# One attention stage, 1369 steps in a hand-written order: the order written anew in its opening and in its last list

## The chip, the cores and the metric

The kernel runs on one core of a Trainium2 chip. Its time is the time that the device takes for one execution, in microseconds (us). A core has several engines with an instruction queue each, and each takes its queue in order: PE (TensorE) multiplies and transposes, ACT (ScalarE) copies, scales and takes exponentials, DVE (VectorE) adds, subtracts and reduces, POOL (GpSimd) and SP (SyncE) here mostly issue DMAs. They wait for one another through semaphores. An engine that stands at an instruction whose input or output buffer isn't ready holds back all that is behind it in its queue, ready or not.

## The reference

One step of a streaming encoder layer, for 1024 prompt tokens and 32 sample tokens with a cache of 512. The part that matters here is branch A, multi-head latent attention with eight heads: queries come from a latent of rank 384, keys and values from one of rank 256, and a rotated key part (krope, 32 wide) is shared by all heads.

```python
q = (rms_norm(q_lat, g_q_lat) @ w_uq).reshape(B, T, H_A, NOPE + ROPE)
q_nope, q_rope = q[..., :NOPE], apply_rope(q[..., NOPE:], cos, sin)
k_rope = apply_rope(k_r, cos, sin)            # also an output of the layer
k_nope, v = c_kv @ w_uk, c_kv @ w_uv          # per head, 64 + 64
s = (einsum('bqhd,bshd->bhqs', q_nope, k_nope) + einsum('bqhr,bsr->bhqs', q_rope, k_rope)) * MLA_SCALE
p = softmax(where(kpos // CHUNK <= qpos // CHUNK, s, NEG))
o_a = einsum('bhqs,bshd->bqhd', p, v)
merged = g_a * (o_a @ w_proj_a) + g_b * (o_b @ w_proj_b)
```

`o_b` is the other branch, finished earlier. The sample's 32 tokens attend to the cache and to themselves.

## The kernel before

All data are float32. A product is made of three matmuls: each operand is split into a high half (rounded, ACT, L68) and a low half (the rest, DVE, L71), and `mm3` multiplies high by high (L75), low by high (L76) and high by low (L77).

The stages follow one another: constants, the common projection, the other branch, the latents, latent attention (`stage_mla`, about 573 to 830 us), the merge of the branches, the feed-forward net. Latent attention takes its eight heads in four pairs; the work of a pair is a *list*, 0 to 3. In a pair, query blocks of 128 go against the keys that they may see.

The order of the work in this stage is written out by hand: `ORDER_M` is a string of tokens, and `mla_attend` takes them one by one and calls a small step for each. The stage runs with a manual schedule for PE, ACT and DVE, so the order of the tokens is the order on those three engines; the orders of POOL and SP follow from the tiles. A token's first digit says whose step it is, its letter which, a last number (as in `f2`) how often it is taken. The tokens that matter:

- `9…`: the first expansion. 9z, 9x, 9y are matmuls for rotated queries, plain queries and keys (352, 352 and 512 columns), 9A a block of values (12 matmuls of 256), 9c and 9d the high and low half of a value block (L1568, L71), 9B the rotation of queries (L1479, its last two issue stores), 9X and 9K the copies of the queries of the two heads (DVE L1498, ACT L1496), 9H/9g and 9L/9b the halves of the keys, 9R and 9r the halves of the key rows that come from krope (`KH<-A`, `KL<-A`), 9J and 9j those of the queries. 9t turns krope for its output (three transposes, L1394), and 9n copies it to a buffer `nat` (L1397, L1398) and stores it with seven POOL DMAs.
- no digit: the other branch's product with `w_proj_b`, of which steps are strewn among the lists: Q fetches its operand, e and l split it (`ObH`, `ObL`), U, W and w load and split weights, f is a product of three matmuls of 264 columns, G copies a finished tile to `nat` (L1889) and stores it to `pbd` (POOL, L1890). There are two `nat` buffers, for 9n and all G together.
- `0…` to `3…`: a list's own steps. S scores (L1619 to L1624), M, m, n maxima, E exponential (L962), R, c, C the scale, T transposes (L806), h and v the halves of the transposed weights (`PTh`, `PTl`, or `ptd` on the diagonal), V the product with the values (L820), o and p its copy and sum (L792, L794). In list 3, q and r split the result for the next stage.
- 3Y: one of the 32 steps of the sample's attention (`mla_sample`), strewn over list 3. In each of its two halves come scores, maximum, exponential, scale, transposes and copies (L1789), product with the cache (L1795), copy (L1798), a last product (L1804; the 31st 3Y in the second half) and its copies `os` (L1809) with their store to `oa` (POOL, L1811; the 32nd).

Behind the last token `stage_mla` loads the attention's result back (`big<-oa`, SP, L1678) as three operands (k = 1, 2, 0), splits them to `QH`/`QL`, `KH`/`KL` and `QH`/`QL`, splits the weights `w_proj_a` (`wh<-KSm`, `wl<-KSm`), and begins the next stage's product with them (352 columns). These steps stand outside the manual schedule: they go where the scheduler puts them, in among the last tokens too.

Of the kernel before, what the change touches and what calls it, by code (L numbers as in the profile page):

```python
# [44 lines left out]
class K:  # L45
# [802 lines left out]


    ORDER_M = """  # L850
        9A 9z 9z 9z 9c 9d 9z 9z 9B 9z 9B 9z 9z 9c 9B 9B 9z 9y 9B 9y 9H 9x 9x 9B 9g 9x 9X 9K 9d 9A 9R 9c 9x 9c 9x
        9r 9y Q 9x 9L 9x 9X 9d 9b 9y 9g 9H Q 9x 9x 9d 9A 9X 9b 9A 9J 9c 9K 9c 9L Q W 9j 9d 0S1.0 9d w 9K 9c Q e
        0M1.0 e l e 0n1.0 0E1.0 l 0S0.0 0M0.0 e 0S1.1 f 9c l 9t 0n0.0 0E0.0 f 9d l 9d 0R0.0 0S2.0a f W 0c0.0
        0S0.1 f G f 0M0.1 0R1.0 f 0n0.1 0E0.1 f2 w 0R0.1 0c1.0 0M1.1 G 9n 0S2.0b 0C0.1 0n1.1 0M2.0b 0E1.1 f
        0M2.0a 0R1.1 f 0m2.0 f 0T0.0 f 0D 0h0.0 f 0E2.0a 0v0.0 0C1.1 0S2.1a 0E2.0b G 9J f 0M2.1a 0S2.1b 0S3.0b
        0V0.0 f 0M2.1b 0m2.1 0E2.1b 0T1.0 0s2.0 0T1.1 f 0S3.0a 0E2.1a f 0h1.0 9j f 0M3.0b 0M3.0a G 0R2.0 0m3.0
        0h1.1 0s2.1 0E3.0a 0R2.1 0S3.1b 0v1.1 f 0M3.1b 0E3.0b 0C2.1 f 0S3.1a 0M3.1a f 0m3.1 0c2.0 0o0 0E3.1a 0p0
        f 0S4.0a 0s3.0 f 0T2.0 G 0S4.0b 0V1.1 0M4.0a 0v1.0 f 0E3.1b 0S4.1b 0h2.0 0V1.0 0M4.0b 0s3.1 0m4.0 0I
        0R3.0 0v2.0 0T2.2 0E4.0a 0R3.1 0i 0T2.1 0M4.1b 0h2.2 0o1 0S4.1a 0p1 0z 0z 0M4.1a 0z G 0h2.1 0z 0E4.0b
        0m4.1 0E4.1a 0v2.2 0c3.0 0S5.0b 0V2.2 0S5.0a 0v2.1 0C3.1 0z 0M5.0b 0V2.1 0T3.3 0z 0M5.0a 0V2.0 0B 0B  # L860
        0h3.3 0m5.0 0z 0z 0B 0z 0B 0x U 9Z 0s4.0 9Z 0v3.3 0o2 0T3.1 0E4.1b W 0s4.1 0T3.2 0h3.2 0x 0B 0p2 0B 0x
        0R4.1 0v3.2 0S5.1b 0X 0V3.3 0E5.0b 0h3.1 0V3.2 0v3.1 0E5.0a 0T3.0 0R4.0 0C4.1 0V3.1 0K 0h3.0 0c4.0 0v3.0
        U 0S5.1a 0x 0M5.1b 0S6.1 0V3.0 0T4.3 0x 0o3 0x 0M5.1a 0x 0s5.0 0m5.1 0T4.2 0h4.3 w 0M6.1 0v4.3 0x 0E5.1b
        0X 0K 0p3 0h4.2 0R5.0 0T4.1 0h4.1 0n6.1 0x U 0v4.2 0E5.1a 0E6.1 0V4.3 0s5.1 0c5.0 0X 0K 0V4.2 0T4.0
        0S6.0 0v4.1 0R5.1 0h4.0 f 0C5.1 0J 0v4.0 f 0M6.0 0S7.0 0n6.0 f 0V4.1 0T5.1 0T5.2 0M7.0 0V4.0 f 0h5.1 0j
        0h5.2 G 0y 0v5.2 f 0E6.0 0R6.1 0y 0n7.0 0o4 f 0R6.0 0H f 0E7.0 f 0T5.0 0p4 0C6.1 0c6.0 0L 0S7.1 0h5.0
        0v5.1 0M7.1 0v5.0 0V5.2 0g 1S1.1 W 0T6.1 G 0n7.1 0V5.1 0h6.1 0R7.0 1M1.1 0b 1n1.1 0E7.1 0V5.0 0y 0o5
        0T6.0 1E1.1 0c7.0 0v6.1 0h6.0 1S0.0 0p5 w 0y 1S1.0 1M0.0 f 0R7.1 0C7.1 0g 0V6.1 f 0H f 0T7.0 1S0.1 0v6.0
        0V6.0 W 1n0.0 f 0b 1E0.0 1S2.0b 1M1.0 0L 1R0.0 1n1.0 f w 1M0.1 1n0.1 1c0.0 0h7.0 1M2.0b 1E1.0 0o6 f
        0v7.0 0p6 1S2.0a 1E0.1 1M2.0a f 1R0.1 f 1R1.0 1m2.0 0J 1C0.1 1S2.1b 0V7.0 G G 0j 1R1.1 f 1M2.1b f 1T0.0  # L870
        0o7 1E2.0b f 1C1.1 1S2.1a 1D U 1M2.1a 1E2.0a 1S3.0a 1m2.1 f2 1c1.0 1h0.0 W 0p7 f 1s2.0 1E2.1a 1T1.0
        1E2.1b 1M3.0a 1S3.0b 1S3.1b 1v0.0 w 1M3.0b G 1V0.0 1m3.0 1s2.1 1R2.0 1T1.1 1h1.0 1o0 f 1R2.1 f 1E3.0a
        1h1.1 G f 1M3.1b 1p0 1S3.1a 1E3.0b f 1c2.0 1v1.0 1k f 1v1.1 1M3.1a 1s3.0 1m3.1 1C2.1 1V1.1 1V1.0 1S4.0a
        1T2.2 f 1E3.1a 1o1 1E3.1b 1p1 1S4.0b 1T2.1 1M4.0a f 1h2.2 1s3.1 G 1R3.0 1R3.1 f 1v2.2 1h2.1 1c3.0 1S4.1b
        1M4.0b f 1v2.1 1T2.0 1m4.0 1C3.1 1V2.2 f 1E4.0a 1h2.0 1S4.1a 1T3.3 1M4.1b 0Z 1v2.0 1I 1V2.1 1V2.0 1M4.1a
        1E4.0b 1m4.1 1h3.3 1v3.3 1E4.1b 1o2 1i 1s4.0 1T3.2 1E4.1a 1S5.0a 1S5.0b 1T3.1 1x 1h3.2 1S5.1b 1p2 1R4.0
        1M5.0b G 1s4.1 1R4.1 1N 1c4.0 1x 1V3.3 1M5.0a 1m5.0 1x 1v3.2 1V3.2 1M5.1b 1x 1C4.1 1E5.0b 1h3.1 1T3.0
        1v3.1 1S5.1a 1X 1E5.0a 1x 1M5.1a 1m5.1 1h3.0 1s5.0 1K 1S6.0 1R5.0 1v3.0 1M6.0 1E5.1b 1T4.3 1E5.1a 1c5.0
        1x 1h4.3 1V3.1 1V3.0 0Z 1T4.2 1x 1X a 1s5.1 1n6.0 1o3 U Q 1h4.2 1K 1v4.3 1R5.1 1E6.0 1C5.1 1v4.2 1p3
        1R6.0 1c6.0 1x 1x 1X 1Z 1J 1j 1K Q 1T4.1 f2 1h4.1 f2 G 1V4.3 1V4.2 1T4.0 1S6.1 1v4.1 1h4.0 1S7.0 f 1y  # L880
        1v4.0 1T5.2 1M7.0 1h5.2 1n7.0 1M6.1 1V4.1 1v5.2 1V4.0 1E7.0 1n6.1 1T5.1 1o4 1h5.1 1E6.1 1y f 1T5.0 f 1H
        1p4 1v5.1 1S7.1 1R7.0 1h5.0 1R6.1 1C6.1 f 1V5.2 1L 1g 1v5.0 1V5.1 1c7.0 2S0.1 1T6.1 e 1M7.1 1b 1V5.0 W
        2M0.1 1n7.1 l 1T6.0 1h6.1 2n0.1 1y 1o5 1p5 1v6.1 1y 1E7.1 1h6.0 1v6.0 1R7.1 2S0.0 2E0.1 1C7.1 8S 1V6.1
        1H 1V6.0 8s a 2S2.0b 1o6 2M0.0 a 2n0.0 G 1T7.0 1h7.0 1p6 1L 2S1.0 8A 2M2.0b 2R0.1 2M1.0 1g 2E0.0 2n1.0
# [30 lines left out]
        3T7.0 G 3v6.0 3h7.0 f 3V6.0 3r f 3v7.0 3o6 3q 3Y 3p6 3r 3V7.0 3o7 f 3Y 3q f3 3p7 3r f 3q f G G 3r
# [1806 lines left out]
```

## Time and profile before

| | us |
|---|---|
| median of three runs (lowest, highest) | 1691.21 (1689.96, 1692.04) |
| the profiled execution | 1692.0 |
| its span in the trace | 1690.2 |
| PE busy in the span | 1647.4 (97%) |
| DVE, ACT, POOL busy | 1268.7, 1007.4, 299.2 |
| from 573 to 835 us: PE busy | 253.43 of 262 |

A row of a timeline gives the start in us from the span's start, the duration in us, the engine, the line, the operation, output tile <- input tiles and the shape; at its end, in brackets, how long the engine had been idle before and what released it. `x4` joins four equal neighbours. A matmul's duration runs over that of the next: its cost to PE is the distance from its start to the next one's. A row of the waits gives the engine, the line and tile that waited, the engine, tile and line that it waited for, then the sum in us, the count, and the longest. A row of the windows gives a stretch of time and the engines' busy time in it. PEclk is the clock that was granted to PE, as a share of full speed.

### The profile page before, as it was taken

To read this page: it belongs to the slowest core of one execution; us is meant where nothing else is said; L and a number is where in the kernel's file an instruction comes from. 1 tells how busy PE (TensorE), PEld (TensorE's weight loads), DVE (VectorE), ACT (ScalarE), POOL (GpSimd) and SP (SyncE) were. 2 spreads that over 40 slices of the span, in tenths; PEclk is the share of its full clock that TensorE was granted. 3 is DMA by queue.
4 is the path that set the end of the run, shared out by engine and by line. 5 is a ranking of instruction groups with operands and counts; after the bars stand their busy time and mean duration, and the time that the engine had idled before them with its cause. 6 is when DMAs were issued, how large, how long until landed. Compare 5 with 4: busy or idle time off the path is not lost. (4 is left out here: it accounts for less than half of the span.)

```text
span 1690.2 us, 30269 instructions
## 1 busy us (share of the span) xinstructions
PE 1647.4 (97%) x11592; PEld 1511.3 (89%) x11592; DVE 1268.7 (75%) x2140; ACT 1007.4 (60%) x1945; POOL 299.2 (18%) x581
## 2 busy tenths in 40 slices
...
DMA packets 194145, 260.62 MB, mean 154 GB/s; under 512 B 23374, under 2 KB 132304, under 8 KB 193936
## 3 DMA queue, kind: packets, MB, share of 16 engines
...
q14 instruction: 54, 0.44, 0.1%
...
## 5 line engine op out<-in xcount | busy, mean ns | idle before, releaser
L68 ACT ACTIVATE wh<-wr 128x1024 fp32r<-128x1024 f32 (+2 forms) x151 | 130.2, 864 | 231.7 <-PE s L2176 83.2
L71 DVE TENSOR_TENSOR wl<-wr,wh 128x1024 fp32r<-128x1024 f32 (+2 forms) x151 | 148.3, 985 | 79.3 <-ACT wh L68 78.9
L75 PE MATMUL mm<-hh,wh 128*128 128x352 f32 x456 | 152.6, 335 | 0.1
L76 PE MATMUL mm<-hl,wh 128*128 128x352 f32 x456 | 148.6, 326 | 0.1
L77 PE MATMUL mm<-hh,wl 128*128 128x352 f32 x456 | 148.4, 325 | 0.0
L2175 PE MATMUL mm<-T,wh 128*128 128x256 f32 (+1 forms) x376 | 108.2, 288 | 0.0
L2177 PE MATMUL mm<-T,wl 128*128 128x256 f32 (+1 forms) x376 | 107.2, 286 | 0.6 <-DVE wl L71 0.5
L2176 PE MATMUL mm<-T,wh 128*128 128x256 f32 (+1 forms) x376 | 106.7, 284 | 0.0
L2177 PE MATMUL s<-T,wl 128*128 128x256 f32 (+1 forms) x348 | 99.3, 285 | 0.0
L2175 PE MATMUL s<-T,wh 128*128 128x256 f32 (+1 forms) x348 | 99.3, 285 | 0.0
L2176 PE MATMUL s<-T,wh 128*128 128x256 f32 (+1 forms) x348 | 98.8, 284 | 0.0
L71 DVE TENSOR_TENSOR wl<-S,wh 128x1024 fp32r<-128x1024 f32 (+1 forms) x55 | 59.2, 1077 | 51.7 <-ACT wh L68 51.4
L75 PEld LDWEIGHTS mm<-hh,wh 128*128 128x128 f32 x456 | 86.4, 190 | 3.7 <-issue 2.1
L2316 DVE SCALAR_TENSOR_TENSOR u<-u,c,u 128x1058 f32<-128x1058 f32 x68 | 87.0, 1317 | 1.9 <-ACT u L2313 0.7
L76 PEld LDWEIGHTS mm<-hl,wh 128*128 128x128 f32 x456 | 86.5, 190 | 2.2 <-DVE hl L333 0.7
L806 PE MATMUL tr<-c,A 128*128 128x128 f32 x576 | 86.7, 272 | 0.6 <-DVE ptd L71 0.6
L77 PEld LDWEIGHTS mm<-hh,wl 128*128 128x128 f32 x456 | 86.3, 189 | 0.6 <-issue 0.4
L68 ACT ACTIVATE wh<-S 128x1024 fp32r<-128x1024 f32 (+1 forms) x55 | 51.8, 943 | 47.9 <-PE s L2176 13.4
L2175 PE MATMUL tr<-T,wh 128*128 128x272 f32 (+1 forms) x272 | 77.8, 286 | 0.0
L2177 PE MATMUL tr<-T,wl 128*128 128x272 f32 (+1 forms) x272 | 77.7, 286 | 0.0
L2176 PE MATMUL tr<-T,wh 128*128 128x272 f32 (+1 forms) x272 | 77.3, 284 | 0.0
L71 DVE TENSOR_TENSOR PTl<-tr,PTh 128x512 fp32r<-128x512 f32 x96 | 65.5, 686 | 11.8 <-ACT PTh L68 11.0
...
## 6 DMA issues: line engine op xcount, KB each, us to landing
...
```

The costliest lines, as they stand in the source:

```text
L68: self.nc.scalar.activation(out, in_, AF.Identity, scale=scale)
L71: return self.nc.vector.tensor_tensor(out, full, hi.bitcast(F32), ALU.subtract)
L75: m(ps, lh, rh, start=start, stop=False)
L76: m(ps, lh, rl, start=False, stop=False)
L77: self.pe = m(ps, ll, rh, start=False, stop=stop).ins
L806: self.nc.tensor.transpose(tr[:, (2 * s + q) * P : (2 * s + q + 1) * P], at[q][:, b * P : b * P + P], self.idt)
L2175: m(ps[:, :n], w[0][:, k], x[0][:, k, c], start=first and k == 0, stop=False, skip_group_check=True)
L2176: m(ps[:, :n], w[0][:, k], x[1][:, k, c], start=False, stop=False, skip_group_check=True)
L2177: i = m(ps[:, :n], w[1][:, k], x[0][:, k, c], start=False, stop=k == 3, skip_group_check=True)
L2316: nc.vector.scalar_tensor_tensor(y, u[:, w : w + YW], self.cvT[:, w, cc : cc + 1], y, ALU.mult, ALU.add)
```

## The change

The change replaces tokens of `ORDER_M` in two stretches: the opening (the first 333 tokens, which are 328 afterwards) and the end of list 2 with list 3 (the last 404, now 402). The 632 tokens between stay word for word. The steps are the same in number and kind; some single f become f2 or f4. No other line changes. Of the table's diff, its first lines:

```diff
     ORDER_M = """
-        9A 9z 9z 9z 9c 9d 9z 9z 9B 9z 9B 9z 9z 9c 9B 9B 9z 9y 9B 9y 9H 9x 9x 9B 9g 9x 9X 9K 9d 9A 9R 9c 9x 9c 9x
+        9z 9z 9z 9z 9z 9z 9B 9z 9y 9z 9z 9B 9B 9x 9B 9A 9x 9A 9B 9x 9B 9c 9x 9x 9y 9d 9X 9c 9c 9R 9d 9c 9x 9g Q
```

ACT in the expansion, first before and then after: the copies of the second head's queries (L1496) and the key rows (`KH<-A`), among halves of values (L1568) and keys.

```order
L1568 ACTIVATE V_7006<-mm_7016 128x4x64
L1568 ACTIVATE V_7007<-mm_7016 128x4x64
L68 ACTIVATE KH_6987<-mm_7068 64x512
L68 ACTIVATE KH_6989<-mm_7068 64x512
L1496 ACTIVATE big_7094<-s_7078 64x352
L68 ACTIVATE KH_6987<-A_6222 64x1024
L1568 ACTIVATE V_7006<-s_7100 128x4x64
L1568 ACTIVATE V_7007<-s_7100 128x4x64
```

```order
L1568 ACTIVATE V_7007<-mm_7060 128x4x64
L1568 ACTIVATE V_7006<-s_7076 128x4x64
L68 ACTIVATE KH_6987<-A_6222 64x1024
L1568 ACTIVATE V_7007<-s_7076 128x4x64
L68 ACTIVATE KH_6989<-mm_7043 64x512
L68 ACTIVATE KH_6987<-mm_7043 64x512
L1496 ACTIVATE big_7111<-s_7055 64x352
L1496 ACTIVATE big_7111<-s_7097 64x352
```

The key rows stood behind the first of these query copies; now all three query copies stand behind the key rows and the first key halves.

ACT at the krope output (L1397, L1398) and the first copies of finished tiles (L1889), before and after; all of them write the two `nat` buffers.

```order
L971 ACTIVATE A_7221<-A_7221,sum_7223 128x128
L1889 COPY nat_7282<-mm_7239 128x264
L962 ACTIVATE A_7271,sum_7273<-s_7274,mx_7272,lat_6225 128x256
L971 ACTIVATE A_7197<-A_7197,sum_7199 128x384
L1889 COPY nat_7306<-mm_7285 128x264
L1397 COPY nat_7309<-tr_7245 128x256
L1398 COPY nat_7309<-tr_7245 8x128
L962 ACTIVATE A_7231,sum_7233<-s_7234,mx_7232,lat_6225 128x512
```

```order
L68 ACTIVATE KH_6989<-s_7151 64x512
L1568 ACTIVATE V_7006<-s_7162 128x4x64
L1397 COPY nat_7187<-tr_7145 128x256
L1398 COPY nat_7187<-tr_7145 8x128
L1568 ACTIVATE V_7007<-s_7162 128x4x64
L68 ACTIVATE ObH_7223<-A_7124 128x528
L68 ACTIVATE ObH_7223<-A_7155 128x528
L68 ACTIVATE wh_6993<-wr_7010 128x512
L962 ACTIVATE A_7198,sum_7200<-s_7201,mx_7199,lat_6225 128x256
```

The krope copies stood behind two L1889; now they stand ahead of the first one, inside the expansion.

ACT at the end of the sequence, before and after: the last diagonal weights (`ptd`), the copies of results (L792), and the next stage's operands `KH<-big` (k = 2) and `QH<-big` (k = 0) and weights `wh<-KSm` (of which before has the first just ahead of these rows).

```order
L68 ACTIVATE ptd_6982<-tr_10417 128x384
L792 COPY o_10439<-pv_10412 64x256
L68 ACTIVATE V_9588<-o_10398 64x256
L792 COPY o_10454<-pv_10449 64x256
L68 ACTIVATE V_9588<-o_10439 64x256
L68 ACTIVATE V_9588<-os_9739 128x32
L68 ACTIVATE V_9588<-o_10454 64x256
L1889 COPY nat_10482<-mm_10426 128x264
L68 ACTIVATE wh_10547<-KSm_10508 128x512
L1889 COPY nat_10485<-mm_10466 128x264
L68 ACTIVATE KH_6987<-big_10500 128x1056
L68 ACTIVATE QH_10494<-big_10504 128x1056
```

```order
L1889 COPY nat_10421<-mm_10374 128x264
L68 ACTIVATE KH_6987<-big_10500 128x1056
L68 ACTIVATE ptd_6982<-tr_10430 128x384
L792 COPY o_10443<-pv_10425 64x256
L68 ACTIVATE V_9577<-o_10399 64x256
L68 ACTIVATE QH_10494<-big_10504 128x1056
L1889 COPY nat_10463<-mm_10439 128x264
L68 ACTIVATE wh_10513<-KSm_10508 128x512
L792 COPY o_10466<-pv_10457 64x256
```

`KH<-big` and `QH<-big` stood behind all steps of the list; now they stand among the last of them, `KH<-big` right ahead of the last `ptd`. On DVE the low halves `KL<-big` and `QL<-big` stand in the same places: `KL` right ahead of the last `ptd`, `QL` ahead of `wl<-KSm`.

In the tokens, the sample's last two steps (31st and 32nd 3Y) stood 17 and 11 places from the end (`3o6 3q 3Y 3p6 3r 3V7.0 3o7 f 3Y 3q f3 3p7 3r f 3q f G G 3r`), and stand 73 and 64 places from it now, ahead of the scores of the last block and half of the last products with the values. The other thirty are spread anew over list 3.

More of the change, by code (lines that the diff above doesn't have):

```diff
@@ L856 @@
[L856 to L860, printed above, removed]
@@ new lines @@
+        9x 9x 9x 9H 9K 9d 9r 9X 9K 9L 9t 9X 9K 9y Q 9y 9J 9A 9H 9d 9b 9j 9L Q Q 9g 9c 9n 9b 0S0.1 9c 0M0.1 9A 9d
+        9d e e W 0n0.1 0E0.1 l l w e 0S1.0 e 0S0.0 0M0.0 W l l 0n0.0 0M1.0 0E0.0 0S1.1 0n1.0 0M1.1 f2 0R0.1
+        0R0.0 f2 G 0n1.1 0C0.1 0S2.0a f 0E1.0 9c 0M2.0a 0c0.0 f 0S2.0b 9d 0E1.1 0M2.0b 0R1.0 0m2.0 w 9c f2 0T0.0
+        0E2.0a 0R1.1 0E2.0b 9d 0S3.0a 0s2.0 0C1.1 0S2.1a 0h0.0 0S2.1b f2 0R2.0 f 0M2.1a G 0c1.0 0T1.0 0v0.0 f2
+        0M2.1b 9J U 0m2.1 0E2.1b 0M3.0a 0D 9j f 0E2.1a G 0h1.0 f 0S3.0b f 0V0.0 0M3.0b G 0m3.0 0S3.1b 0E3.0a
@@ new lines @@
+        0s2.1 f 0o0 0v1.0 0T1.1 f 0M3.1b 0S3.1a f 0R2.1 0M3.1a f 0m3.1 0E3.0b 0c2.0 0C2.1 0h1.1 f2 0E3.1a f
+        0s3.0 f 0p0 0T2.1 0S4.0b 0S4.0a 0v1.1 0E3.1b 0I 9Z G 0S4.1b 0V1.1 0R3.0 0s3.1 0M4.0b 0V1.0 0i 0h2.1
+        0M4.0a 0T2.2 0c3.0 0o1 0z 0z 0h2.2 0z G 0m4.0 0E4.0b 0v2.1 0T2.0 0M4.1b 0R3.1 0p1 0z 0h2.0 0v2.2 0C3.1
+        0S4.1a 0M4.1a 0v2.0 0m4.1 0V2.2 0E4.0a 0T3.3 0h3.3 0S5.1b 0v3.3 0V2.1 0V2.0 0M5.1b 0T3.2 0E4.1a 0z 0T3.1
+        0B 0h3.2 0z 0B 0S5.0a 0E4.1b 0z 0h3.1 0v3.2 0o2 0s4.0 0B 0B 0R4.0 0S5.0b 0x 0s4.1 0z 0p2 0M5.0b 0c4.0 W
@@ new lines @@
+        0R4.1 0V3.3 0V3.2 0z 0M5.0a 0m5.0 0v3.1 0E5.0b 0x 0T3.0 0h3.0 0V3.1 0x 0B 0B 0C4.1 0E5.0a 0S5.1a 0T4.3
+        0v3.0 0T4.2 0V3.0 0X 0x 0h4.3 0v4.3 0M5.1a 0m5.1 0o3 0x 0S6.1 0p3 0h4.2 0T4.1 0E5.1a 0h4.1 0V4.3 0v4.2
+        0K 0V4.2 0M6.1 0x 0E5.1b 0s5.0 0R5.0 0X 0s5.1 0n6.1 w 0R5.1 0x 0x 0x 0X 0T4.0 0v4.1 0c5.0 0K 9Z 0h4.0
+        0E6.1 0S6.0 f 0C5.1 0J U 0v4.0 f 0M6.0 0S7.0 0n6.0 f U 0K 0V4.1 0T5.1 0T5.2 0M7.0 0V4.0 f 0h5.1 0j 0h5.2
+        G 0y 0v5.2 f 0E6.0 0R6.1 0y 0n7.0 0o4 f 0R6.0 0H f 0E7.0 f 0T5.0 0p4 0C6.1 0c6.0 0L 0S7.1 0h5.0 0v5.1
@@ new lines @@
+        0M7.1 0v5.0 0V5.2 0g 1S1.1 W 0T6.1 G 0n7.1 0V5.1 0h6.1 0R7.0 1M1.1 0b 1n1.1 0E7.1 0V5.0 0y 0o5 0T6.0
+        1E1.1 0c7.0 0v6.1 0h6.0 1S0.0 0p5 w 0y 1S1.0 1M0.0 f 0R7.1 0C7.1 0g 0V6.1 f 0H f 0T7.0 1S0.1 0v6.0 0V6.0
+        W 1n0.0 f 0b 1E0.0 1S2.0b 1M1.0 0L 1R0.0 1n1.0 f w 1M0.1 1n0.1 1c0.0 0h7.0 1M2.0b 1E1.0 0o6 f 0v7.0 0p6
+        1S2.0a 1E0.1 1M2.0a f 1R0.1 f 1R1.0 1m2.0 0J 1C0.1 1S2.1b 0V7.0 G G 0j 1R1.1 f 1M2.1b f 1T0.0 0o7 1E2.0b
+        f 1C1.1 1S2.1a 1D U 1M2.1a 1E2.0a 1S3.0a 1m2.1 f2 1c1.0 1h0.0 W 0p7 f 1s2.0 1E2.1a 1T1.0 1E2.1b 1M3.0a
@@ new lines @@
+        1S3.0b 1S3.1b 1v0.0 w 1M3.0b G 1V0.0 1m3.0 1s2.1 1R2.0 1T1.1 1h1.0 1o0 f 1R2.1 f 1E3.0a 1h1.1 G f 1M3.1b
+        1p0 1S3.1a 1E3.0b f 1c2.0 1v1.0 1k f 1v1.1 1M3.1a 1s3.0 1m3.1 1C2.1 1V1.1 1V1.0 1S4.0a 1T2.2 f 1E3.1a
+        1o1 1E3.1b 1p1 1S4.0b 1T2.1 1M4.0a f 1h2.2 1s3.1 G 1R3.0 1R3.1 f 1v2.2 1h2.1 1c3.0 1S4.1b 1M4.0b f 1v2.1
+        1T2.0 1m4.0 1C3.1 1V2.2 f 1E4.0a 1h2.0 1S4.1a 1T3.3 1M4.1b 0Z 1v2.0 1I 1V2.1 1V2.0 1M4.1a 1E4.0b 1m4.1
+        1h3.3 1v3.3 1E4.1b 1o2 1i 1s4.0 1T3.2 1E4.1a 1S5.0a 1S5.0b 1T3.1 1x 1h3.2 1S5.1b 1p2 1R4.0 1M5.0b G
@@ new lines @@
+        1s4.1 1R4.1 1N 1c4.0 1x 1V3.3 1M5.0a 1m5.0 1x 1v3.2 1V3.2 1M5.1b 1x 1C4.1 1E5.0b 1h3.1 1T3.0 1v3.1
+        1S5.1a 1X 1E5.0a 1x 1M5.1a 1m5.1 1h3.0 1s5.0 1K 1S6.0 1R5.0 1v3.0 1M6.0 1E5.1b 1T4.3 1E5.1a 1c5.0 1x
+        1h4.3 1V3.1 1V3.0 0Z 1T4.2 1x 1X a 1s5.1 1n6.0 1o3 U Q 1h4.2 1K 1v4.3 1R5.1 1E6.0 1C5.1 1v4.2 1p3 1R6.0
+        1c6.0 1x 1x 1X 1Z 1J 1j 1K Q 1T4.1 f2 1h4.1 f2 G 1V4.3 1V4.2 1T4.0 1S6.1 1v4.1 1h4.0 1S7.0 f 1y 1v4.0
+        1T5.2 1M7.0 1h5.2 1n7.0 1M6.1 1V4.1 1v5.2 1V4.0 1E7.0 1n6.1 1T5.1 1o4 1h5.1 1E6.1 1y f 1T5.0 f 1H 1p4
@@ L915 @@
[L915 removed]
+        2R5.1 2x 2v4.2 2K f 2X 2R6.0 2Z 2K 2c5.0 2J f 2Z 2V4.2 2T4.0 2C5.1 2c6.0 2h4.0 2v4.1 2j 2S6.1 2y 2M6.1
+        2n6.1 2v4.0 2V4.1 2T5.0 2h5.0 2S7.0 2y 2E6.1 2T5.2 2V4.0 2H 2h5.2 2o4 2v5.0 2R6.1 2T5.1 2M7.0 2C6.1 2L f
+        2p4 2n7.0 2S7.1 2v5.2 2M7.1 2h5.1 2g f G 3S0.1 2J 2V5.2 f2 2v5.1 f 2b f 2V5.1 2E7.0 2n7.1 W 2T6.1 2V5.0
+        2j 2h6.1 2o5 2R7.0 w 2v6.1 2T6.0 3M0.1 f 3S0.0 2p5 2E7.1 2R7.1 f G 3M0.0 2h6.0 2C7.1 2V6.1 3n0.1 f 2y
@@ new lines @@
+        2v6.0 3n0.0 2c7.0 f 2y 3S1.0 3E0.0 2V6.0 3E0.1 G 2T7.0 3S1.1 f4 3S2.0b 3Y 3R0.0 2H 3c0.0 U 3R0.1 3M1.0
+        3C0.1 2L 3n1.0 3M1.1 2g 2h7.0 2o6 3E1.0 3R1.0 W 3S2.0a 3c1.0 3Y 2v7.0 2p6 2V7.0 2b 3n1.1 3E1.1 3T0.0
+        3M2.0b w 3R1.1 3Y 3M2.0a 3m2.0 3h0.0 3Y 2o7 3E2.0a 3S2.1a 3E2.0b G 3C1.1 3v0.0 f 3Y 2p7 3S2.1b 3s2.0 3Y
+        3M2.1b 3M2.1a 3V0.0 3m2.1 3Y 3T1.1 3o0 3E2.1b 3T1.0 3h1.1 3h1.0 f 3v1.1 3Y f 3E2.1a f 3v1.0 3Y 3s2.1
+        3R2.0 3Y 3S3.0a 3p0 3c2.0 f 3q f2 3V1.1 3R2.1 3S3.0b 3C2.1 3Y 3T2.1 3h2.1 3Y 3M3.0b 3Y f 3S3.1b 3V1.0
@@ new lines @@
+        3M3.0a 3m3.0 3Y 3v2.1 3T2.2 3E3.0b 3Y 3S3.1a 3E3.0a 3o1 3Y 3M3.1b 3S4.0b 3h2.2 W 3r 3M3.1a 3m3.1 3E3.1b
+        3p1 3v2.2 3Y 3T2.0 w 3S4.0a 3M4.0b 3s3.0 3E3.1a 3R3.0 3S4.1a 3Y 3h2.0 3M4.0a 3m4.0 3s3.1 3c3.0 3E4.0b
+        3v2.0 3V2.2 3S4.1b 3V2.1 3R3.1 3C3.1 3q 3T3.3 3Y 3E4.0a G 3T3.2 3V2.0 G 3M4.1b 3M4.1a 3h3.3 3h3.2 3v3.3
+        3Y 3m4.1 3r 3s4.0 3T3.1 3o2 3p2 3E4.1a 3v3.2 3E4.1b 3Y 3s4.1 3h3.1 3R4.1 3V3.3 3R4.0 3V3.2 3C4.1 3c4.0
+        3v3.1 3q 3Y 3T3.0 3T4.3 3V3.1 3S5.0a 3h3.0 f 3v3.0 3T4.2 3V3.0 3h4.3 3Y 3h4.2 3M5.0a 3v4.3 3o3 3S5.1b
```

56 lines of the change are left out of this document (9 added, 47 removed).

## The prediction

> **What bounds the kernel now.** I read the page's first two parts, then PE's waits in the attention stage, then its busy time and clock in stretches.
>
> ```profile
> PE 1647.4 (97%) x11592; PEld 1511.3 (89%) x11592; DVE 1268.7 (75%) x2140; ACT 1007.4 (60%) x1945; POOL 299.2 (18%) x581
> PE mm L75 <- ACT KH L68: 2.8, 1, 2.8
> PE s L1619 <- ACT A L962: 2.1, 1, 2.1
> PE s L75 <- DVE V L71: 2.0, 1, 2.0
> PE pv L820 <- DVE o L794: 0.7, 1, 0.7
> PE tr L806 <- DVE ptd L71: 0.6, 1, 0.6
> PE mm L76 <- DVE ObL L71: 0.4, 1, 0.4
> 580.00:600.00 20.00, 17.47 (x116) 15.42 (x115) 14.49 (x31) 13.91 (x30) 1.75 (x5) 1.00 0.79 189
> 600.00:610.00 10.00, 7.90 (x48) 7.41 (x46) 6.03 (x17) 6.38 (x19) 5.82 (x10) 0.83 0.26 69
> 810.00:820.00 10.00, 10.00 (x75) 8.62 (x75) 7.11 (x22) 8.12 (x21) 0.00 (x0) 1.00 0.01 2
> 830.00:850.00 20.00, 17.10 (x88) 16.52 (x87) 10.11 (x14) 8.81 (x11) 1.54 (x10) 0.83 0.62 225
> ```
>
> PE is the bound (97%). The next six rows are nearly all of its waits from 575 to 850 us: 8.6 us, and three of them, 6.9 us, lie in the opening and at the end of the sequence. The window rows (busy time of PE, PEld, DVE, ACT, POOL, then granted clock, DMA share, GB/s) show full work between, and a second loss: a clock of 0.83 over 10 us is 1.7 us of full speed lost, 0.83 over the 20 us from 830 is 3.4. So 13.7 us is all that better order there can win. The change keeps the work: the same matmuls, copies and DMAs. At 97% PE is the bound in the stages behind as well, so a gain there should reach the end.
>
> **The change, part by part.**
>
> *Opening, front.* The waits of the expansion:
>
> ```profile
> 589.65 0.36 PE L75 MATMUL s<-wh,lat 128*128 128x256 f32 x1 [1.96 <-DVE V L71]
> 585.66 1.22 DVE L71 TENSOR_TENSOR KL<-A,KH 64x1024 fp32r<-64x1024 f32 x1 [2.80 <-ACT KH L68]
> 584.09 0.46 ACT L1496 ACTIVATE big<-s 64x352 f32<-64x352 f32 x1 [2.33 <-DMA rqs<-big]
> 584.58 1.06 ACT L68 ACTIVATE KH<-A 64x1024 fp32r<-64x1024 f32 x1
> 594.20 1.70 ACT L68 ACTIVATE ObH<-A 128x528 fp32r<-128x528 f32 x3
> A<-ob SPq DMA_DIRECT2D x4, 264.0 KB, 8.4
> ```
>
> Read upward: ACT waits 2.33 us for a store (`rqs<-big`) before a query copy (9K), and the key rows (9R, `KH<-A`) stand behind that copy; DVE waits 2.80 us for 9R; the value halves stand behind it on DVE; PE waits 1.96 us for those. In the new order 9R, four value copies and two key copies stand ahead of the first 9K. The same instructions run, so the most it can win is 1.96 + 0.4 (for `ObL`) = 2.4 us. The least is a loss: PE's first f needs `ObH`, which ACT splits from fetches that took 8.4 us to land. If PE comes to it earlier than they do, the gain is a wait again, and a fetch that lands 1 us later than now costs 1. Four scores and a value block now stand ahead of the first f, where three scores stood, which gives the fetches time, so I take most of it: **1.5 us** (-1 to 2.4).
>
> *Opening, krope output.*
>
> ```profile
> 603.91 0.37 ACT L1397 COPY nat<-tr 128x256 f32<-128x256 f32 x1 [2.94 <-DMA pbd<-nat]
> 605.24 0.44 PE L1619 MATMUL s<-KH,QH 128*128 128x384 f32 x1 [2.10 <-ACT A L962]
> ```
>
> Two G stores hold both `nat` buffers, so the copy 9n waits 2.94 us for a landing; exponentials (`A`, L962) queue behind it on ACT, and PE waits 2.10 us for a score bank. Its clock then drops (0.83 above). Now 9t and 9n stand ahead of the first G and ask for no landing. What moves with 9n are its two copies (0.37 us the longer) and seven POOL DMAs, which go ahead of the first G store; at the 0.54 us that POOL takes for the store in the last fence below, seven take 3.8 us, and that store can come so much later, which the two buffers bear unless the third G follows sooner. The wait goes, 2.1 us, and with it the clock loss, 1.7 us: **3.8 us** (0 if the first G pair now waits for POOL, to 3.8).
>
> [...]
>
> Elsewhere in the expansion and list 0 the order is new as well; I charge 1 us for it, two waits of the size of the smaller ones above (0.4 to 0.7). Opening: 1.5 + 3.8 - 1.0 = **4.3 us** (-1.5 to 6.2).
>
> *End of list 3.* The sample's last two steps (the 31st 3Y: product L1804; the 32nd: copies and a store) stand 17 and 11 tokens before the end; their result makes a round trip through memory and is the k = 2 and k = 0 operand of the next stage's product.
>
> ```profile
> 826.00 1.00 PE L1804 MATMUL tr<-big,big 128*128 128x64 f32 x8
> 826.81 0.41 PE L75 MATMUL s<-QH,wh 128*128 128x352 f32 x1
> 827.37 0.65 PE L820 MATMUL pv<-ptd,V 128*128 128x256 f32 x4
> 827.86 0.28 PE L75 MATMUL mm<-ObH,wh 128*128 128x264 f32 x1
> 828.21 0.28 PE L75 MATMUL mm<-ObH,wh 128*128 128x264 f32 x1
> 821.59 0.60 PE L806 MATMUL tr<-c,A 128*128 128x128 f32 x4
> 821.94 0.37 PE L75 MATMUL mm<-ObH,wh 128*128 128x264 f32 x1
> 827.59 0.46 DVE L1809 COPY os<-tr 64x64 f32<-64x64 f32 x2
> 828.34 0.54 POOL L1811 DMA_DIRECT2D oa<-os  x1 [2.84 <-DVE os L1809]
> 830.21 0.85 SPq L1678 DMA_DIRECT2D big<-oa  x2
> 834.15 1.08 ACT L68 ACTIVATE KH<-big 128x1056 fp32r<-128x1056 f32 x1 [3.16 <-DMA big<-oa]
> 835.27 1.26 DVE L71 TENSOR_TENSOR KL<-big,KH 128x1056 fp32r<-128x1056 f32 x1 [3.81 <-ACT KH L68]
> 835.68 1.09 ACT L68 ACTIVATE QH<-big 128x1056 fp32r<-128x1056 f32 x1 [0.44 <-DMA big<-oa]
> 835.29 0.96 PE L75 MATMUL mm<-KH,wh 128*128 128x352 f32 x2 [2.79 <-ACT KH L68]
> 825.09 0.49 ACT L68 ACTIVATE ptd<-tr 128x384 fp32r<-128x384 f32 x1
> 826.21 0.55 DVE L71 TENSOR_TENSOR ptd<-tr,ptd 128x384 fp32r<-128x384 f32 x1
> 830.76 0.69 DVE L71 TENSOR_TENSOR wl<-KSm,wh 128x512 fp32r<-128x512 f32 x1 [0.88 <-ACT wh L68]
> 828.45 0.43 DVE L794 TENSOR_TENSOR o<-pv,o 64x256 f32<-64x256 f32 x1 [0.40 <-ACT o L792]
> 828.80 0.41 DVE L71 TENSOR_TENSOR V<-o,V 64x256 fp32r<-64x256 f32 x1
> 593.55 0.36 PE L1619 MATMUL s<-KH,QH 128*128 128x256 f32 x1 [0.16 <-DVE V L71]
> 594.11 0.39 PE L1619 MATMUL s<-KH,QH 128*128 128x512 f32 x1
> ```
>
> From L1804's start to the landing of the first load is 834.15 - 826.00 = 8.15 us, of the second about 9.65. Before, PE ran out and waited 2.79 us; then came the 3.4 us of lost clock. Those 6.2 us are the prize.
>
> Now they stand 73 and 64 tokens before the end. PE's work behind L1804, by the steps of the rows (pv 0.12, transposes 0.09, an f 0.36, L1804 0.81): up to the last transposes (T7.0) 24 pv, 18 transposes, 5 f, a score (593.55 to 594.11): 0.8 + 2.9 + 1.6 + 1.8 + 0.55 = 7.7 us. The loads thus land at 8.15, half a microsecond behind T7.0. And here the new order is dearer: ACT has `KH<-big` right ahead of the last `ptd<-tr`, and DVE `KL<-big` ahead of its half. ACT: 8.15 + 1.08 + 0.49; DVE: KL from about 9.3 to 10.5, then 0.55: 11.0. PE has 4 pv and 4 f more, to 9.6, so it waits about 1.4 us for the last values. Then the weights: DVE does `o` 0.43, a split of it 0.41, `QL<-big` 1.26, `o` and split again, and only then `wl` 0.69: 11.0 + 3.6 = 14.6, where PE's last pv, four f and six products of the next stage end at 11.0 + 0.5 + 1.4 + 1.0 = 13.9: 0.7 us more. With 0.1 for hand-overs the new waits are 2.2 us; each is under 2.1, so I leave the clock whole. Gain 6.2 - 2.2 = **4.0 us**. Ends: 6.2 if no wait appears; 0.6 if the clock dips all the same (-3.4). The waits for `o` and `ptd` (0.7, 0.6) lie in the part that is written anew and may stay or go.
>
> *Sum.* 4.3 + 4.0 = 8.3 us off the profiled 1692.0, which is 0.8 above the median of the runs, 1691.21: 1683.7 or 1682.9. I say 1683.5.
>
> **Rivals.**
>
> *Only one end wins.* The waits at the end are moved into the list rather than removed: KH, QH, KL and QL stand among the last steps, where before they stood behind them. With 2.2 us of new waits and 3.4 of clock 0.6 is left there: 1692.0 - 4.3 - 0.6 = 1687.1. Or the opening loses its gain to the A fetches and the end keeps 4.0: 1688.0.
>
> *The clock loss is not the waits'.* If a gap as short as these does not take the clock down and something else does, the 1.7 and 3.4 us stay, and the sum is 8.3 - 5.1 = 3.2: 1688.8. For it: the 1.96-us gap that cost nothing. Against: both slow stretches begin right behind a wait of over 2 us. [...]
>
> *No change.* Both ends at their small values, 0.6 and about 0.5: 1691. For it: a DMA share of 0.62 as the next stage begins (830:850), where earlier products may only meet later fetches. Against: the only long wait there is for `KH`, not for a fetch.
>
> *Slower: the sample's chain inside list 3.* The other 30 steps are spread anew over the list too. Each step on PE needs the ACT or DVE step before it, and PE takes its turn in order: a step that comes too soon stops all scores behind it. Row 810:820 says that PE has no slack to give back there. Twelve waits of the size of `pv` (0.7), or two like krope's with its clock (2.1 + 1.7 = 3.8 us each) and one of 0.7, eat the 8.3 us; three and one of 0.7 make 1695.5. Against: four neighbouring pairs of 3Y now stand 2 or 3 tokens apart, five stood 1 to 3 apart before, and before shows a single wait of 0.6 us there.
>
> **How the numbers follow.** Both ends at half their gain or more, 0.58: 1683.5, own range 1679 to 1687.5. Only one end: 0.15, at 1687 to 1688. The clock's loss stays: 0.06, at 1688.8. No change: 0.08. Slower: 0.13. About 0.2% (3.4 us) is what a measurement of this kernel can tell from no change, so against 1691.21 faster means below 1687.8. To the 0.58 come four fifths of the 15 of only one end: faster 0.70; the rest of it, the clock's case and no change make same 0.17; slower 0.13. Range: from the sum of the best ends (6.2 + 6.2, 1692.0 - 12.4 = 1679.6, less a little for the two waits that may go) to 1691.5; what lies above is the slower case and little else.
>
> **What would show it.** Right: no `pbd<-nat` ahead of L1397, no 2-us wait before the first f, clock at 1.00 from 590 to 615 and behind the list's end; PE waits of 1 to 1.5 us before the last pv and for `wl<-KSm`. Wrong: PE waits for L1789, L1798 or `big` between 775 and 815; a wait above 2 us at the last `ptd`; a low clock in either place.

## The result, and the profile after

The changed kernel takes 1686.34 us (median of ten runs, 1684.32 to 1687.97) against 1690.03 us (ten runs, 1687.98 to 1692.04): a ratio of 0.9976 with a 95% interval of 0.9966 to 0.9986, so 2.4 to 5.7 us faster. The forecast had the sign, and the time lies in its range, but it promised 7.7 us against the median then known, and about half of that came. One execution of one experiment (the new list 3 alone) took 5671 us where its other twelve took 1688 to 1692; it is left out, and a second trace stands for that kernel.

First where the time went, by four matmuls on PE that both traces have at the same place of the program: the last product of the stage before (L1376), a product of the middle that both orders share (L1716), the first of the next stage's long product (L1935), and the first of the stage behind (L2143). Timeline of PE, before, then after:

```profile
572.61 0.63 PE L1376 MATMUL mm<-hl,wk 128*32 128x264 f32 x8
723.75 0.39 PE L1716 MATMUL tr<-c,lat 128*32 128x128 f32 x2
853.22 0.42 PE L1935 MATMUL pv<-dh,gs 128*32 128x256 f32 x4
957.19 0.44 PE L2143 MATMUL tr<-c,f 128*128 128x128 f32 x2
```

```profile
570.58 0.63 PE L1376 MATMUL mm<-hl,wk 128*32 128x264 f32 x8
718.64 0.39 PE L1716 MATMUL tr<-c,lat 128*32 128x128 f32 x2
846.19 0.63 PE L1935 MATMUL pv<-dh,gs 128*32 128x256 f32 x7
950.90 0.44 PE L2143 MATMUL tr<-c,f 128*128 128x128 f32 x2
```

The spans differ by 5.1 us (1690.2 and 1685.1). Of that 2.0 us are there before the changed code begins (572.61 against 570.58): the trace of before has a clock of 0.50 from 527.42 to 530.83 us, that of after 1.00 from 500 to 573, and the code is the same. In the second traces below the two kernels stand the other way round at this matmul: 570.85 us for before, 572.47 for the changed kernel. The opening (L1376 to L1716) went from 151.14 to 148.06 us, the end (L1716 to L1935) from 129.47 to 127.55, and behind it 0.75 us came back (103.97 to 104.71). So the change won 3.1 + 1.9 - 0.7 = 4.3 us in this pair. Behind L2143 another 1.2 us came back (733.0 us to the end of the span, against 734.2). I don't count them: that stretch takes 732.9 to 734.5 us in the thirteen traces, whatever the kernel.

PE's waits in the stage after (engine, line and tile that waits, what it waits for, sum, count, longest):

```profile
PE pv L820 <- DVE o L794: 2.9, 4, 1.1
PE mm L75 <- ACT nat L1889: 1.1, 1, 1.1
PE s L1624 <- DVE QL L71: 0.7, 1, 0.7
PE s L1619 <- ACT A L962: 0.5, 1, 0.5
PE s L1619 <- DVE KL L71: 0.3, 1, 0.3
PE s L1619 <- DVE mx L960: 0.3, 1, 0.3
```

All three long waits of before (2.8, 2.1, 2.0) are gone. In the opening 1.8 us of small ones stand in their place, against 4.7 before. At the end there are 4.0 us, against 4.1 (2.8 + 0.7 + 0.6): nothing was won there in waits. The waits for `o` are four, where before had one.

The clock in the opening did drop again, in another place. Timeline of PE, then two windows of the same trace (PE, PEld, DVE, ACT, POOL, granted clock, DMA share, GB/s):

```profile
588.64 0.39 PE L1624 MATMUL s<-KH,QL 128*128 128x256 f32 x1 [0.72 <-DVE QL L71]
590.80 0.41 PE L1619 MATMUL s<-KH,QH 128*128 128x384 f32 x1 [0.34 <-DVE KL L71]
591.95 0.36 PE L1619 MATMUL s<-KH,QH 128*128 128x256 f32 x1 [0.27 <-DVE mx L960]
593.20 0.57 PE L1619 MATMUL s<-KH,QH 128*128 128x512 f32 x1 [0.53 <-ACT A L962]
```

```profile
590.08:593.49 3.41, 2.27 (x13) 1.47 (x12) 3.38 (x8) 3.41 (x10) 2.60 (x4) 1.00 0.55 147
593.49:596.90 3.41, 3.41 (x15) 2.81 (x15) 3.38 (x12) 2.22 (x5) 1.72 (x4) 0.50 0.31 88
```

Three waits of 0.3 to 0.5 us lie in one stretch of 3.41 us, and the next 3.41 us run at a clock of 0.50. No single wait is near 2 us.

At the end of the list, ACT, DVE and PE after:

```profile
818.94 1.28 ACT L1694 ACT_TABLE_LOAD   x1
820.46 0.36 ACT L792 COPY o<-pv 64x256 f32<-64x256 f32 x1
821.34 0.75 PE L820 MATMUL pv<-ptd,V 128*128 128x256 f32 x4 [1.07 <-DVE o L794]
821.90 1.09 ACT L68 ACTIVATE KH<-big 128x1056 fp32r<-128x1056 f32 x1
823.02 1.26 DVE L71 TENSOR_TENSOR KL<-big,KH 128x1056 fp32r<-128x1056 f32 x1 [0.63 <-ACT KH L68]
824.20 0.55 DVE L71 TENSOR_TENSOR ptd<-tr,ptd 128x384 fp32r<-128x384 f32 x1
824.78 0.43 DVE L794 TENSOR_TENSOR o<-pv,o 64x256 f32<-64x256 f32 x1
825.26 0.74 PE L820 MATMUL pv<-ptd,V 128*128 128x256 f32 x4 [0.71 <-DVE o L794]
828.84 0.38 ACT L1889 COPY nat<-mm 128x264 f32<-128x264 f32 x1 [1.09 <-DMA pbd<-nat]
829.27 0.43 PE L75 MATMUL mm<-QH,wh 128*128 128x352 f32 x1 [1.14 <-ACT nat L1889]
```

`KH<-big` no longer waits for its load: it stands in ACT's queue behind the load of a function table (1.28 us, L1694, the first thing that the next stage asks of ACT), and the last values behind it wait 0.71 us as `KL` and `ptd` pass through DVE. The third wait is for a `nat` buffer whose store landed late, 6.5 us after its issue, while the next stage's fetches run beside it. The clock was 1.00 there, from 815 to 846 us.

### The profile page after: what moved, and what is told of

It reads as the page before. It is cut to its first block, busy times and chain, and to the rows that moved or that the text cites. A ratio compares the mean times of both kernels' runs of the same rounds, so it can differ in the third digit from the quotient of the medians.

```text
span 1685.1 us, 30257 instructions
## 1 busy us (share of the span) xinstructions
PE 1643.0 (97%) x11592; PEld 1506.5 (89%) x11592; DVE 1268.6 (75%) x2140; ACT 1008.5 (60%) x1945; POOL 299.7 (18%) x581
## 5 line engine op out<-in xcount | busy, mean ns | idle before, releaser
L68 ACT ACTIVATE PTh<-tr 128x512 fp32r<-128x512 f32 x96 | 57.0, 599 | 27.3 <-PE tr L806 22.9
```

The source lines that it names most:

```text
L68: self.nc.scalar.activation(out, in_, AF.Identity, scale=scale)
```

## The experiments

The order table is one string, so parts of the change can be taken alone. Three numbers from each trace, by the rows shown above: the opening (start of the last eight L1376 to the first L1716), the end (to the first L1935), the merge (to L2143); "low" is half of the length of the stretches with a clock of 0.50 within (0.5 x 3.41 = 1.7 us each), my estimate from those rows of the most that they cost. Same orders with and without such a stretch show a smaller difference: with 3.41 us of it the opening took 1.3 us more (changed, 148.06 against 146.80), with 6.83 us the end took 2.2 more (before, 129.47 against 127.30, with 4.1 and 4.0 us of waits).

| kernel | opening (low) | end (low) | merge | ratio to before, 95% |
|---|---|---|---|---|
| before | 151.14 (1.7) | 129.47 (3.4) | 103.97 | |
| before, second trace | 151.47 (1.7) | 127.30 (0) | 103.96 | |
| changed | 148.06 (1.7) | 127.55 (0) | 104.71 | 0.9976 (0.9966 to 0.9986) |
| changed, second trace | 146.80 (0) | 127.39 (0) | 104.68 | |
| new opening only | 146.81 (0) | 128.05 (1.7) | 103.96 | 0.9978 (0.9968 to 0.9987) |
| new list 3 only, second trace | 148.13 (0) | 127.12 (0) | 104.17 | 0.9990 (0.9981 to 0.9999) |
| only 9n moved | 153.21 (3.4) | 128.37 (1.7) | 103.96 | 1.0015 (1.0005 to 1.0025) |
| only 9t, 9n moved far | 151.45 (3.4) | 129.02 (1.7) | 103.96 | 0.9994 (0.9985 to 1.0004) |
| only the last two 3Y moved | 151.21 (1.7) | 127.41 (1.7) | 104.24 | 0.9993 (0.9983 to 1.0003) |
| changed, 9A first | 148.05 (1.7) | 126.88 (0) | 104.11 | 0.9971 (0.9960 to 0.9981) |
| before, table load late | 151.20 (1.7) | 127.51 (1.7) | 103.96 | 0.9991 (0.9981 to 1.0002) |
| changed, table load late | 146.80 (0) | 124.88 (0) | 103.96 | 0.9952 (0.9938 to 0.9965) |
| changed, table load last | 146.83 (0) | 124.33 (0) | 103.93 | 0.9957 (0.9945 to 0.9970) |

**Each half alone.** The new tokens of one place, the old of the other.

```diff
     ORDER_M = """
-        9A 9z 9z 9z 9c 9d 9z 9z 9B 9z 9B 9z 9z 9c 9B 9B 9z 9y 9B 9y 9H 9x 9x 9B 9g 9x 9X 9K 9d 9A 9R 9c 9x 9c 9x
+        9z 9z 9z 9z 9z 9z 9B 9z 9y 9z 9z 9B 9B 9x 9B 9A 9x 9A 9B 9x 9B 9c 9x 9x 9y 9d 9X 9c 9c 9R 9d 9c 9x 9g Q
...
```

> Before with only the new opening (expansion and list 0), list 3 as before. Theory A (the two places are independent and add up): between the end of the previous stage and the last product of list 0 this stage is about 3.0 us shorter than before, as in the changed kernel, the krope wait of 2.1 us and the wait of 1.96 us are gone, and the end keeps its wait of 2.8 us for KH and its half clock: the whole is 2.5 to 3.5 us faster than before. Rival B (a clock window that moves): the half-clock stretch falls elsewhere, so the opening wins 4.5 us or the end loses some; the whole differs from 3 us by 1.5 us or more.

> Before with only the new list 3, opening as before. Theory A: the opening keeps its waits of 1.96 and 2.10 us and the low clock behind them; the end wins 2.0 us, as in the changed kernel, with no half clock behind the list and waits of about 1 us each for o behind the table load, for the last o, and for a nat buffer: 1.5 to 2.5 us faster than before. Rival C (the end's gain is given back, since the next stages wait for fetches in its place): within 0.5 us of before.

> The kernel of the new list 3 alone once more, for its trace: the first execution shown was one of several milliseconds, which no other run repeats. [...]

The opening alone wins 4.4 us against the old order's usual 151.2, and its whole ratio is that of the full change. It also shows what a trace of after hid: with the same order and nearly the same waits (0.7, 0.7 in two, 0.4, 0.3) this execution kept its clock (1.00 from 580 to 620 us), and the opening is 1.25 us shorter than after's. So rival B is right that the clock moves, though in the good direction: its 4.5 us came in the opening, but the whole, 3.7 us (2.2 to 5.4), lies nearer to theory A's 3 than B said.

The new list 3 alone is a little faster: 0.9990, that is 1.7 us (0.2 to 3.2), in theory A's range but too uncertain to shut out rival C. Its trace gives the end as 127.12 us, with a whole clock and the waits of the changed kernel (3.0 us for `o` in four, 0.7 for `nat`). This trace held a surprise in the old opening, though:

```profile
602.52 0.37 ACT L1397 COPY nat<-tr 128x256 f32<-128x256 f32 x1 [1.09 <-DMA pbd<-nat]
603.86 0.44 PE L1619 MATMUL s<-KH,QH 128*128 128x384 f32 x1 [0.26 <-ACT A L962]
```

The krope wait, 2.94 us on ACT and 2.10 on PE in the trace of before, is 1.09 and 0.26 here, and no low clock follows. The instructions are the same; the first store landed 2.2 us after its issue (600.28 to 602.44) where in the trace of before it took 4.0 (599.83 to 603.83).

**Both kernels a second time**, for what an execution draws anew.

> The kernel before, unedited, for a second trace. The old order gave a krope wait of 2.10, 1.95 and, once, 0.26 us on PE, since the store that it waits for landed after 4.0, 3.8 and 2.2 us. Theory K (the price of the old opening is drawn anew in each execution): this trace falls near one of the two, 150.9 us from the last L1376 to the first L1716 with a low clock, or 148 without, and 128 to 129.5 us from there to the first L1935. Rival L (2.1 us is the rule and 0.26 came from the other kernel's list): 150.9 us.

> The changed kernel, unedited, for a second trace. [...]

The old opening is the costly one again (2.3 us for the krope wait), in four of the five traces that have it. The old end is another story. A row of its waits, and the window behind:

```profile
PE mm L75 <- ACT KH L68: 2.5, 1, 2.5
```

```profile
829.52:832.94 3.42, 1.82 (x10) 1.42 (x9) 0.69 (x1) 0.54 (x3) 0.62 (x2) 1.00 0.83 266
832.94:836.35 3.41, 2.17 (x12) 1.88 (x13) 1.95 (x2) 2.79 (x3) 0.20 (x2) 1.00 1.01 395
```

The wait for `KH` is nearly as long as in the first trace, and this time it fell half into one window of 3.41 us and half into the next (1.82 and 2.17 us of PE's time used; the windows are counted in steps of 3.41 us from this trace's low stretch at 604.24): the clock is 1.00 in both, and the end took 127.30 us, as long as with the new list 3. With the old list the end had 3.4, 0, 1.7, 1.7 and 1.7 us of low clock in five traces; with the new one none, in four.

The changed kernel's second trace has an opening of 146.80 us and an end of 127.39, both with a whole clock. The idle time in the window is nearly the same in the two: 1.05 us here (3.41 - 2.36, in 589.28:592.69), with a clock of 1.00 in the next window, and 1.14 (3.41 - 2.27) in the first trace, with 0.50 in the next.

**The krope copy alone**, first just ahead of the first G, then far ahead.

```diff
-0S1.1 f 9c l 9t 0n0.0 0E0.0 f 9d l 9d 0R0.0 0S2.0a f W 0c0.0 0S0.1 f G f ... G 9n 0S2.0b
+0S1.1 f 9c l 9t 0n0.0 0E0.0 9n f 9d l 9d 0R0.0 0S2.0a f W 0c0.0 0S0.1 f G f ... G 0S2.0b
```

> Before with one token moved: the krope copy 9n stands right behind the second exponential of list 0, ahead of the first G, its transposes stay. Theory A: ACT's wait of 2.94 us for a landing and PE's of 2.10 us go, and the half-clock stretch near 606 with them: 2.1 + 1.7 = 3.8 us less by the end of list 0, so this one token wins more than the whole new opening did (3.0). Rival D: another wait stands right behind (the exponentials wait for maxima or a score bank) and PE keeps about 1 us or the low clock: 1 to 2 us less.

This failed on both theories: the kernel became slower. Its ACT and PE:

```profile
606.29 0.38 ACT L1889 COPY nat<-mm 128x264 f32<-128x264 f32 x1 [4.25 <-DMA out_dram<-nat]
606.72 0.59 PE L75 MATMUL mm<-ObH,wh 128*128 128x264 f32 x1 [2.65 <-ACT nat L1889]
```

Now the second G waits for a buffer, 4.25 us, since the krope copy holds one until its last store has landed, and its seven DMAs (599.62 to 603.95 on POOL) also stand ahead of the first G's store. The one buffer shortage is paid by whoever comes third: 9n before, G here.

```diff
-9A 9X 9b 9A 9J 9c 9K 9c 9L Q W
+9A 9X 9b 9A 9t 9J 9n 9c 9K 9c 9L Q W
```

> Before with the krope transposes and copy (9t, 9n) moved into the expansion, next to the first QH, some 10 us ahead of the first G; all else as before. Theory G (two buffers and three users: it counts how far the copy is from the G pair, not on which side of it): neither ACT's wait of 2.94 us nor the 2.7 us of G behind the copy is there, PE's 2.1 us and the low clock behind it go: 3.5 to 4 us less by the end of list 0, where the copy 1.5 us ahead of the first G cost 2 us. Rival H: the seven POOL DMAs and the copies in the crowded expansion delay the key rows and QH, and 1 us or more of that is paid there.

The G pair waits for no buffer now, but the price came up elsewhere, by rival H's kind of mechanism with another cause:

```profile
591.15 0.36 PE L75 MATMUL s<-wh,lat 128*128 128x256 f32 x1 [2.46 <-DVE V L71]
596.13 0.37 ACT L1397 COPY nat<-tr 128x256 f32<-128x256 f32 x1 [3.61 <-PE tr L1394]
```

ACT stood 3.61 us at the copy, as PE had the three transposes late, and the clock was 0.50 twice, from 592.51 to 595.92 us behind PE's wait of 2.46 and from 599.34 to 602.75. Of the two places tried for the copy alone neither won anything; the opening's gain came with the new order of the expansion as a whole, which moves key rows, blocks and transposes together. Which of these moves is needed was not tried.

**The block ahead of the score.** In the changed kernel PE waits 0.72 us for `QL` inside the first score, and a block of 12 matmuls stands right behind.

```diff
-Q Q 9g 9c 9n 9b 0S0.1 9c 0M0.1 9A 9d 9d e e W
+Q Q 9g 9c 9n 9b 9A 0S0.1 9c 0M0.1 9d 9d e e W
```

> The changed kernel with its last value block 9A moved ahead of the first score 0S0.1 (it stood right behind it). Theory A': the block's 1.43 us hide the 0.72 us that PE waits for QL, so the window that held 1.91 us of idle (and lost 1.7 us of clock) or 1.73 us (and lost none) holds about 1.2 and no window phase takes the clock down: the opening ends 0.7 us earlier than with the same order and a whole clock (4.3 against before), that is 5 us ahead of before in every run; the whole 0.7 to 2 us faster than the changed kernel. Rival F: the wait moves (exponentials or maxima come as late as they did), the idle time stays at 1.7 to 1.9 us, the opening stays at 3.1 to 4.3 us.

```profile
591.17 0.41 PE L1619 MATMUL s<-KH,QH 128*128 128x384 f32 x1 [1.38 <-DVE KL L71]
```

Rival F: the wait for `QL` went, and the next score waits 1.38 us for `KL` where it waited 0.34. PE was not what was late here; DVE's chain to `KL` is, and 0.72 + 0.34 us became 1.38. The low clock came again (0.50 from 593.51 us), behind a window of which PE used 1.61 us. The expectation's 1.91 and 1.73 us of idle time in the windows of the two older traces are too high: their rows give 1.14 and 1.01 (3.41 - 2.40).

**The last two 3Y alone.** They move next to T5.1 and T5.0; the rest of the old list stays.

```diff
-3R6.0 3n7.1 3T5.1 3T5.0 3o4 ... 3o6 3q 3Y 3p6 3r 3V7.0 3o7 f 3Y 3q f3 3p7 3r f 3q f G G 3r
+3R6.0 3n7.1 3Y 3T5.1 3Y 3T5.0 3o4 ... 3o6 3q 3p6 3r 3V7.0 3o7 f 3q f3 3p7 3r f 3q f G G 3r
```

> Before with only the sample's last two steps moved, to the places next to the transposes T5.1 and T5.0; the rest of list 3 stays in its old order. Theory A (the old order's end wait and clock are the prize, the rest of the new list 3 costs some of it): the wait of 2.79 us and 3.4 us of half clock go, about 2 us of new waits for the last ptd, for wl and for a nat buffer come: 4 us faster by the first k = 3 product, where the new list 3 won only 2. Rival E (the new waits are the price of drawing the steps forward, whatever the rest does): about 2 us faster, as the new list 3.

The end takes 127.41 us, 2.1 less than in the first trace of before and 0.1 more than in the second, and the time of the whole is not told from before (0.9983 to 1.0003). By the number it is rival E. But it holds 1.7 us of low clock (0.50 from 831.00 to 834.42), behind a single wait of 1.8 us for `o`; its waits are 3.0 us (2.2 for `o`, 0.6 for `ptd`, 0.2 for `os`) where the new list has 4.0. So theory A is right that the rest of the new list adds waits, though they stand at `o` and not where it named them, and it has the clock wrong. By this one trace the two steps take the wait for `KH` away, and the other thirty, spread anew, bring nothing of their own.

**The table load.** The load L1694 is tied to the last exponential; here it is tied to `QH<-big` instead, or to the last split of the first weights. The scheduler then also moves one `wh<-KSm` ahead.

```diff
         for k in ks:
...
-            self.hi(self.xh[k], f)
+            late = nc.scalar.activation(self.xh[k], f, AF.Identity, scale=1.0).ins
...
-        with self.tc.issue_after(self.exp.ins):
+        with self.tc.issue_after(late):
             nc.scalar.activation(z, self.epsc, AF.Sigmoid)
```

> The changed kernel with the load of the next stage's function table (L1694, 1.28 us on ACT) tied to the last operand split QH<-big in place of the last exponential. Theory I: the wait of 1.07 us for o behind the table load goes; the table load then delays the last copy of o, wh and the last G by 1.3 us, and PE's wait there (1.14 us for a nat buffer) grows by less than 1: 0 to 1 us faster from L1716 to the first L1935. Rival J (the end is set by the nat buffer's store that lands among the next stage's fetches): the wait for it grows by the whole 1.07 us and nothing is won.

> The changed kernel with the table load behind all splits of the next stage's first weights (behind the list's last copies too). Theory I: the last copy of o, wh and the last G lose the 1.3 us that they still waited for the load: PE's waits of 0.4 us for QH and 0.3 for a nat buffer shrink, 0 to 0.7 us faster than with the load tied to QH<-big, so 1682.5 to 1683.5 us. Rival N: the load now delays the next stage's first copies (L2005) and PE waits for them: 0.5 us slower than that.

> Before with the table load L1694 tied to the last operand split QH<-big in place of the last exponential; the order table is the old one. Theory I: the load goes behind the list, PE's wait of 0.7 us for o goes, the long wait for KH stays, since it hangs on the sample's last steps: 0.5 to 1 us faster than before. Rival M (KH's wait grows by what the list wins, since the chain from the sample's last step to its operand is what ends last): within 0.3 us of before.

With the new list the end falls by 2.7 and 3.2 us against the first trace of after, more than theory I allowed, and the kernels are the fastest here: 1683.23 and 1683.62 us, 0.9952 and 0.9957 of before; the two can't be told apart, and rival N's loss behind the list does not show (a merge of 103.93). PE's waits at the end of the first of them:

```profile
PE pv L820 <- DVE o L794: 1.2, 2, 0.8
PE s L75 <- ACT QH L1679: 0.4, 1, 0.4
PE mm L75 <- ACT nat L1889: 0.3, 1, 0.3
```

Of 4.0 us 1.9 are left. The wait for `o` behind the load went; the last values, which waited 0.71 us behind `KL`, no longer wait, since ACT comes about 1 us earlier to what stands behind the load; and the wait for `nat` shrank to 0.3. Rival J is out. The waits make 2.1 of the 2.7 us; where the rest came from, the runs do not show. The 0.7 us of the merge also went (103.96); but the new list without this edit has 104.11 and 104.17 in two other traces, so that this came of the edit is not shown. With the old list the same edit takes the wait for `o` away and leaves 2.4 us for `KH`; the end is 127.51 with 1.7 of low clock, 0.5 to 1.5 us less than old ends with the same (128.05 to 129.02). The wait for `KH` did not grow, as rival M had it; but by its ratio, 0.9981 to 1.0002, the kernel is not told from before.

## Why the prediction was right or wrong

*Opening, 4.3 us forecast.* By the usual traces of the two orders, 151.2 against 146.8, it is 4.4; by the profiled pair 3.1. The krope wait went as forecast (2.1 us), and the front gave 0.5 to 0.7 after its new small waits (forecast 1.5 - 1.0). What failed is "and with it the clock loss": the clock is not tied to that wait alone. The old opening lost it in the four traces of five in which the krope wait was 1.9 to 2.3 us long, and kept it where the wait was 0.26. But in the trace of after a low stretch stands behind new waits of 0.3 to 0.5 us, and in four other traces of the same opening it doesn't. With such a stretch the opening took 1.3 us more here, where the forecast had 1.7. The forecast is right on the whole and wrong in this execution, which shows one of its own signs of being wrong, a low clock in the opening.

*End, 4.0 us forecast.* This is the term that was mis-sized: it measured 1.9 in the profiled pair, and by the means of the traces (128.4 with the old list in five, 127.2 with the new in four) 1.2. The failed step is "those 6.2 us are the prize". The wait for `KH`, 2.5 to 2.8 us, was there each time, but the 3.4 us of low clock were the worst of five draws of 0 to 3.4, mean 1.7, and as time they cost less than that sum says: the trace of before with them ends 2.2 us later than the one without (129.47 against 127.30, with waits of 4.1 and 4.0 us). The low stretch began at 834.62, while PE still waited (to 835.29), and not behind the wait, as the forecast reads it. So the prize was 2.8 + 2.2 = 5.0 us in the worst trace, and 2.7 + 1.1 = 3.8 by the mean of five (128.4 against 127.3). The new waits were forecast as 2.2 us, at the last values and at the weights; they came there, as 0.71 and 1.14 in after, though the second for a `nat` buffer in place of `wl`, 1.85 in all (1.43 in the second trace, where the wait for `nat` is 0.69). The other half of the failure is the sentence that the waits for `o` and `ptd` "may stay or go", counted at nothing: 1.3 us before, 2.2 after, half of it the table load, which I had left in the order without a price. So old and new wait equally long (4.1 and 4.0 us), and what was won at the end in this pair is the clock: the new list's end (126.9 to 127.6) is no shorter than the one old end without a low stretch (127.30).

*Base.* The profiled 1692.0 was the top of ten runs of 1687.98 to 1692.04: it held the worst end and a clock of 0.50 from 527.42 to 530.83 us. The 0.8 us that the forecast allowed for it should have been 2.0.

*Rivals.* "Only one end wins" is nearest by its time, 1687.1, but not by its reason: at the end the clock was won and the waits were not. "The clock loss is not the waits'" is half true: the eleven low stretches whose windows were read stand behind one in which PE used 1.05 to 2.27 of the 3.41 us, but equal waits had it in one execution and not in another (2.27 us used in after, 2.28 with the late table load). The chain of 3Y inside list 3 stopped nothing for long: the longest of PE's waits there is 0.8 us, for `o`. The slower rival's long waits stand in none of these traces.

*Check by means.* Opening -3.6 (five traces each: 150.6, 147.1), end -1.2, merge +0.5 (103.96 and, in the four traces with the new list, 104.42) give -4.3 us; the ratio, 0.24% of 1690.03, says -4.1 (2.4 to 5.7).
